# Turning attention weights by transposing transfers, with the pairs of heads spread over gates and u

## The chip, the cores and the metric

The kernel runs on one core of one Trainium2 chip. Its time is the device time of one execution in microseconds (us), the median of three runs. The engines are TensorE (PE, with its weight loads as PEld), VectorE (DVE), ScalarE (ACT), GpSimd (POOL) and SyncE (SP), which only issues DMAs here. DMAs that GpSimd issues stand in POOL's queue.

## The reference

Two layers, each of which is `x <- LN(alpha*x + 0.5*SwiGLU_1(x))`, `x <- LN(alpha*x + Mixer(x))`, `x <- LN(alpha*x + 0.5*SwiGLU_2(x))`, for 256 tokens of 1024 numbers, in float32. The change touches the mixer:

```python
z = x @ w_in
u, v, q, k, val, gates = jnp.split(z, SPLITS, axis=-1)
u, v = gelu(u), gelu(v)
# branch A: LN(v), then per group g of 8 a lower triangular 128x128 product over the positions of a chunk
s = jnp.einsum('gtr,bnrgc->bntgc', w, vb) + b_s.T[None, None, :, :, None]
h_a = u * s
# branch B: 8 heads, two softmaxes each; q and k of 64, val of 128 per head
q, k = rope(q), rope(k)
p = softmax(where(causal, q @ k.T * 64 ** -0.5, neg))
a = p[:, :, 0] - lam * p[:, :, 1]
o = a @ val
h_b = rmsnorm(o, diff_ln_g) * (1.0 - lam_init)
g = sigmoid(gates + gate_b)
m = g[:, :, 0] * (h_a @ w_branch[0]) + g[:, :, 1] * (h_b @ w_branch[1])
return m @ w_out
```

## The kernel before

**Precision.** Every large product runs in float32r with the weights cut into a high and a low part. `stream` (line 150) loads 1 MB of weights (128 x 2048) into one of four `raw` buffers; ACT writes the high part `whi` (line 169), DVE the low part `wlo` (line 171), in pieces of 1024 columns, of which eight buffers each exist. Activations stand as a high and a low half in one tile of 512.

**TensorE's order.** The order on TensorE is the order in which the program is written (`manual_schedule`); the other engines' orders are made by a scheduler from priorities, which grow with the order of the program, and from its own model of the times. `issue_after` (in `behind`) puts an instruction behind a named one on its engine: `emptied` is the last eviction of a bank on ACT, `added` the last addition of two halves on DVE, `turned_by` the last rope product on POOL, `loaded` the last load of weights on SP.

**Beats and side tasks.** Small work is written as generators beside the large products. `beat(w)` (line 123) advances a clock; a task whose due time has come runs up to its next `yield d`, and is due again d later, at the next beat that reaches it. `beside(task, delay)` enters a task. `gemm_a2` (line 234) takes one or two loads; for each of its loads it runs two pieces of eight 512-wide matmuls with the high part (line 244), with a beat of 0.65 after each piece, and then for each piece eight 256-wide matmuls with the low part (line 251) and a beat of 0.35. One load is thus two beats. `gemm_b` (line 273) advances the clock by 0.5 for every six matmuls (line 232).

**The mixer** (line 572) has these stages. `val` first; then four pairs of heads, each with a product for q and one for k and `rope` behind each; then eight products for the gates, one v (two halves), four u, then the products with the branch weights, `branch(1, hb)` and `branch(0, ha)`, of eight loads each, and `w_out`. Beside them:

- `attend(hp, qT, kT)` (line 607), one task per pair of heads, entered when its k is done with a delay of 4.5. `scores` uses four `side` banks, two for the second 128 tokens and two for the first. DVE and ACT make the two softmaxes, `less` (line 639) subtracts them on DVE. After 2.9 beats TensorE transposes the weights (lines 658 and 663), six blocks of 128 x 128 in two side banks, ACT evicts them to `aT`. After 1.9 more TensorE multiplies by the values (lines 671 and 673) into one side bank, ACT copies it to `on` (line 676) and squares the bank in place for the sums of the norm (line 681). POOL works out the reciprocal roots (`rsqrt4`, line 214), ACT scales `on` (line 690).
- `transposed` (line 175) turns `on`: POOL parts the two 16-bit halves of the numbers into two planes (line 186), SP issues one transposing DMA per plane (line 190), POOL joins the planes (line 194). ACT and DVE then write high and low part of `hb` (lines 700 and 702).
- `spatial(gp, uu)` (line 750), entered three beats after each u: four products per group pair into one side bank (line 756), then DVE adds the bias and multiplies by u (lines 761 and 763), ACT and DVE split the result into `ha` (lines 197 and 198).
- After v, DVE normalises `vg` (lines 735 and 737). POOL's queue loads `sgug` and `sgub` (line 407), `wsT` and `bsb` (lines 743 and 746), and POOL clears the upper triangle of `wsT` (line 744).

There are four `main` banks for the large products and four `side` banks. Tiles of 512 columns come from one pool, `act`, of 27 slots.

Of the kernel before, what the change touches and what calls it, by code (L numbers as in the profile page):

```python
# [20 lines left out]
P = 128  # L21
# [32 lines left out]
def trunk(ctx, tc, x, xT, w13a, w13b, w2, wb, wqk, wa, wbr, wo, gateb, sgug, sgub, sguwT, sgubias, lam, diffg,  # L54
# [41 lines left out]

    def t512(s, n=2):
        return tmp.tile([P, 512], F32, tag="main", name=name(s), bufs=n)
# [75 lines left out]

    def transposed(src, out, via, first, second):

        def planes(v):
            return v.bitcast(U16).rearrange("p (w c) -> p w c", w=2)  # L180

        def numbers(v):
            return v.bitcast(U16).rearrange("p (c w) -> p w c", w=2)

        for w in range(2):
            G.tensor_copy(out=planes(out)[:, w], in_=numbers(src)[:, w])  # L186
        yield first
        with behind(loaded[0]):
            for w in range(2):
                nc.sync.dma_start(planes(via)[:, w].rearrange("p (k t) -> p k t", k=4), planes(out)[:, w],  # L190
                                  transpose=True)
        yield second
        for w in range(2):
            G.tensor_copy(out=numbers(out)[:, w], in_=planes(via)[:, w])  # L194

# [321 lines left out]
    def ffn(l, f, i, norm, last=False):  # L517
# [18 lines left out]
        def turned(n, t, s, p, wait):  # L536
            yield from transposed(s, p[:, 0], p[:, 1], wait, 0.6)
# [34 lines left out]
    def mixer(l, i, norm):  # L572
# [13 lines left out]

        def rope(src, scale, last=False):

# [10 lines left out]
            def rest():  # L599
                with behind(None if last else added[0]):  # L600
                    V.tensor_tensor(out=r, in0=r, in1=sw, op=ALU.add)
                yield 0

            beside(rest(), 1.25 if last else 1.55)
            return r

        def attend(hp, qT, kT):
# [30 lines left out]

            def less(t, pp):

                nk = (t + 1) * P
                for j in range(2):
                    s = slice(j * nk, (j + 1) * nk)
                    V.scalar_tensor_tensor(out=pp[0][:, s], in0=pp[1][:, s], scalar=c4[:, t * 2 + j : t * 2 + j + 1],
                                            in1=pp[0][:, s], op0=ALU.mult, op1=ALU.add)
                return pp[0]

# [3 lines left out]
            V.scalar_tensor_tensor(out=c4, in0=rc, scalar=neg_lam[l], in1=sums[:, :4], op0=ALU.mult, op1=ALU.mult)  # L651
            second, first = less(1, second), less(0, first)
            yield 2.9
            b = side_bank()
            for j in range(2):
                for c in range(2):
                    o = (j * 2 + c) * P
                    PE.transpose(b[:, o : o + P], second[:, o : o + P], ident)  # L658
            aT1 = slots("aT", 2)[0]
            A.activation(aT1, b, AF.Copy)  # L660
            b = side_bank()
            for j in range(2):
                PE.transpose(b[:, j * P : (j + 1) * P], first[:, j * P : (j + 1) * P], ident)  # L663
            aT0 = slots("aT", 2)[0][:, :T]
            A.activation(aT0, b[:, :T], AF.Copy)
            yield 1.9
            b = side_bank()
# [11 lines left out]
            for q in range(4):  # L679
                s = slice(q * P, (q + 1) * P)  # L680
                A.activation(b[:, s], b[:, s], AF.Square, accum_out=ss[:, q : q + 1])
            yield 2
            with behind(turned_by[0]):
                G.tensor_tensor(out=ss, in0=s2, in1=ss, op=ALU.add)
            r = rsqrt4(ss, 1.0 / (2 * HD))
            yield 2
            for q in range(4):
                s = slice(q * P, (q + 1) * P)
                with behind(emptied[0]):
                    A.activation(on[:, s], on[:, s], AF.Copy, scale=r[:, q : q + 1])  # L690
            yield 1
            moved = slots("moved", 2)[0]
            yield from transposed(on, moved, on, 10, 0.3)
            yield 0.3
            dl = dgs[:, l : l + 1]
            for j in range(2):
                hi, lo = (hb[hp * 2 + j][:, o : o + T].rearrange("p (t c) -> p t c", t=NT) for o in (0, T))
                f = moved.rearrange("p (t j c) -> p j t c", t=NT, j=2)[:, j]
                with behind(emptied[0]):
# [5 lines left out]
        for hp in range(HEADS // 2):  # L705
            qT = rope(wqk[l, hp, 0], HD ** -0.5)
            kT = rope(wqk[l, hp, 1], 1.0, hp == HEADS // 2 - 1)
# [12 lines left out]

        vg = [act.tile([P, 2, 512], F32, tag="val", name=name("vg"), bufs=2) for _ in range(NT)]
        vst = [sm("vst", 12, bufs=2) for _ in range(NT)]
        for h in range(2):
# [3 lines left out]
            gemm_b(wb[l, V_, h], KT, xh, xl, got_v)  # L727
        g_bc, b_bc = bc_load(sgug[l], vst[0][:, :1]), bc_load(sgub[l], vst[0][:, :1])
        for t in range(NT):
            mv = sm("mv", 2)  # L730
            V.bn_aggr(out=mv, in_=vst[t])
            r = rsqrt(mv[:, 1:2], EPS)
            for h in range(2):
                s = slice(h * 512, h * 512 + 512)
                V.scalar_tensor_tensor(out=vg[t][:, h], in0=vg[t][:, h], scalar=mv[:, 0:1], in1=g_bc[:, s],
                                        op0=ALU.subtract, op1=ALU.mult)
                V.scalar_tensor_tensor(out=vg[t][:, h], in0=vg[t][:, h], scalar=r, in1=b_bc[:, s],
                                        op0=ALU.mult, op1=ALU.add)
        wsT, bsb = slots("wsT", 4), slots("bsb", 4)
# [9 lines left out]

        def spatial(gp, uu):  # L750
            b = side_bank()
# [11 lines left out]
            V.tensor_tensor(out=s1, in0=s1, in1=uu, op=ALU.mult)  # L763
# [122 lines left out]
```

## Time and profile before

| | |
|---|---|
| median of three runs | 1224.38 us (1224.3 to 1224.41) |
| time of the profiled execution | 1224.37 us |
| its span, from the first to the last instruction | 1222.4 us |
| granted clock of TensorE | 1.0 |
| busy PE, DVE, ACT, POOL | 99%, 72%, 58%, 22% of the span |

How to read it: L12 is line 12 of the kernel. A timeline row has start and length in us, the engine, the line, the operation, the names out<-in, the shape and the number of instructions merged; in brackets stands the idle time of the engine before it and what ended that. A group row ends in busy us, mean ns of one instruction, and the idle time before them. Matmuls overlap in the array and their ends are modelled, so two starts give a truer interval than a length. A row of DMAs ends in the median us from issue to landing. A window row has the length, then the busy us and number of instructions of PE, PEld, DVE, ACT and POOL, the granted clock, the share of the DMA engines' time and GB/s.

### The profile page before, as it was taken

The page shows a single profiled execution, that of the slowest core. Times are in us where ns is not written, and L with a number is a line of the kernel's source. Part 1 is how long each engine was busy: PE and PEld are TensorE (multiplying, and loading weights), DVE is VectorE, ACT ScalarE, POOL GpSimd, SP SyncE. Part 2 cuts the span into 40 slices and gives each one's busy share as a digit, 9 for nine tenths or more (in the row PEclk, how much of TensorE's full clock was granted, in tenths as well). Part 3 has the DMA queues.
Part 4 walks back from the last instruction along what each step waited for, and adds up shares of the span by engine and source line. Part 5 has one row for each costly group of instructions (what it writes and reads, how often), then busy time and mean ns, then how long its engine had stood idle before and what let it go on. Part 6 is the DMA issues. An engine that isn't in the chain of part 4 may idle for free.

```text
span 1222.4 us, 17217 instructions
## 1 busy us (share of the span) xinstructions
PE 1216.0 (99%) x6127; PEld 1030.1 (84%) x6127; DVE 884.9 (72%) x1500; ACT 710.8 (58%) x1356; POOL 271.8 (22%) x376
## 2 busy tenths in 40 slices
PE   9999999999999999999999999999999999999998
PEld 7888888888888888888888888888888888888887
DVE  7676767886787986766676766678867879676763
ACT  7475446678765555554455564466886655564740
POOL 1433000246400024230023320002462000323200
PEclk9999999999999999999999999999999999999999
DMA  9976645655853746867546757556568456577550
GB/s 345 307 217 231 245 174 185 229 176 169 283 198 138 249 155 215 245 203 258 195 159 205 258 181 258 207 185 204 170 191 277 146 179 235 173 235 238 183 187 35
DMA packets 92902, 254.43 MB, mean 208 GB/s; under 512 B 57568, under 2 KB 58640, under 8 KB 66704
## 3 DMA queue, kind: packets, MB, share of 16 engines
q1 hardware_dynamic: 88848, 240.68, 58.7%
q0 software_dynamic: 3536, 12.13, 3.0%
q8 instruction: 48, 0.79, 0.3%
q10 hardware_dynamic: 432, 0.52, 0.1%
q14 instruction: 38, 0.31, 0.1%
HBM read 235.47 MB, written 1.05 MB: 193 GB/s over the span
## 4 chain that ended last, share of the span: by engine, by line
PE 99%; DMA 0%; DVE 0%; ACT 0%; issue 0%; ACTq 0%
PE bank L232 64%; PE bank L244 19%; PE bank L251 10%; PE bank L347 2%; PE sbank L621 1%; PE sbank L498 1%; PE sbank L673 1%; PE sbank L756 1%; DMA xraw<-in_xT 0%; PE sbank L671 0%; PE sbank L658 0%; PE sbank L663 0%; PE sbank L470 0%; DVE xtok L478 0%; ACT whi L197 0%; DVE st L443 0%
## 5 line engine op out<-in xcount | busy, mean ns | idle before, releaser
L171 DVE TENSOR_TENSOR wlo<-raw,whi 128x512 fp32r<-128x512 f32 (+1 forms) x570 | 523.7, 954 | 137.9 <-ACT whi L169 80.9
L169 ACT ACTIVATE whi<-raw 128x512 fp32r<-128x512 f32 (+1 forms) x570 | 434.5, 800 | 252.5 <-PE bank L232 173.7
L232 PE MATMUL bank<-whi,x 128*128 128x512 f32 x1352 | 420.8, 390 | 0.0
L232 PEld LDWEIGHTS bank<-whi,x 128*128 128x128 f32 x1352 | 253.8, 188 | 52.5
L232 PE MATMUL bank<-wlo,x 128*128 128x512 f32 x676 | 263.1, 389 | 0.0
L244 PE MATMUL bank<-x,whi 128*128 128x512 f32 x768 | 184.6, 392 | 0.0
L244 PEld LDWEIGHTS bank<-x,whi 128*128 128x128 f32 x768 | 141.2, 188 | 28.5
L186 POOL COPY planes<-planes 128x512 uint16<-128x512 uint16 x80 | 85.6, 1096 | 309.0 <-DVE planes L530 309.0
L232 PEld LDWEIGHTS bank<-wlo,x 128*128 128x128 f32 x676 | 126.9, 188 | 26.1
L232 PE MATMUL bank<-whi,hhi 128*128 128x512 f32 (+1 forms) x374 | 141.2, 378 | 0.0
L232 PE MATMUL bank<-wlo,hhi 128*128 128x512 f32 (+1 forms) x374 | 141.0, 377 | 0.0
L232 PE MATMUL bank<-whi,hlo 128*128 128x512 f32 (+1 forms) x374 | 140.9, 377 | 0.0
L251 PE MATMUL bank<-x,wlo 128*128 128x256 f32 x768 | 103.1, 285 | 0.0
L251 PEld LDWEIGHTS bank<-x,wlo 128*128 128x128 f32 x768 | 98.5, 191 | 3.1
L194 POOL COPY planes<-planes 128x512 uint16<-128x512 uint16 x80 | 66.6, 878 | 106.8 <-DMA planes<-planes 106.3
L530 DVE TENSOR_TENSOR planes<-planes,bank 128x512 f32<-128x512 f32 x40 | 27.4, 684 | 87.0 <-issue 71.3
L529 ACT ACTIVATE planes<-bank 128x512 f32<-128x512 f32 x40 | 23.9, 598 | 103.7 <-PE bank L232 102.6
L232 PEld LDWEIGHTS bank<-whi,hhi 128*128 128x128 f32 x374 | 70.4, 188 | 12.9
L232 PEld LDWEIGHTS bank<-wlo,hhi 128*128 128x128 f32 x374 | 70.4, 188 | 12.8
L232 PEld LDWEIGHTS bank<-whi,hlo 128*128 128x128 f32 x374 | 70.4, 188 | 12.8
L597 POOL TENSOR_TENSOR swap<-swap,sin_t 128x512 f32<-128x512 f32 x16 | 27.1, 1692 | 239.8 <-DMA swap<-z 238.1
L252 ACT ACTIVATE r<-bank 128x256 f32<-128x256 f32 x128 | 47.5, 376 | 27.4 <-PE bank L251 27.2
(182 smaller groups left out, 1275.5 us busy)
## 6 DMA issues: line engine op xcount, KB each, us to landing
raw<-in_w13b SPq DMA_DIRECT2D x76, 1024.0 KB, 5.4
raw<-in_w SPq DMA_DIRECT2D x40, 1024.0 KB, 6.3
raw<-in_wa SPq DMA_DIRECT2D x24, 1024.0 KB, 5.6
raw<-in_wb SPq DMA_DIRECT2D x16, 1024.0 KB, 5.0
raw<-in_wqk SPq DMA_DIRECT2D x16, 1024.0 KB, 4.9
raw<-in_wbr SPq DMA_DIRECT2D x16, 1024.0 KB, 5.0
raw<-in_w13a SPq DMA_DIRECT2D x8, 1024.0 KB, 5.2
raw<-in_wo SPq DMA_DIRECT2D x8, 1024.0 KB, 5.0
```

The costliest lines, as they stand in the source:

```text
L169: A.activation(h, r, AF.Copy)
L171: V.tensor_tensor(out=w, in0=r, in1=h.bitcast(F32), op=ALU.subtract)
L186: G.tensor_copy(out=planes(out)[:, w], in_=numbers(src)[:, w])
L194: G.tensor_copy(out=numbers(out)[:, w], in_=planes(via)[:, w])
L232: PE.matmul(ps, xx, w, start=start and n == 0, stop=stop and n == 2)
L244: PE.matmul(b[-1], hi[:, k * P : (k + 1) * P], xc(k), start=k == 0, stop=False)
L251: PE.matmul(b[n][:, :T], lo[:, k * P : (k + 1) * P], xc(k)[:, :T], start=False, stop=k == KT - 1)
L252: emptied[0] = A.activation(r[:, s], b[n][:, T:], AF.Copy, scale=scale).ins
L347: PE.matmul(ps[t][m], x[:, j, o + t * P : o + (t + 1) * P], y, start=k0 + j == 0 and o == 0 and y is hi, stop=k0 + j == KT - 1 and y is lo)
L529: silu[0] = A.activation(s, ps[0], AF.Silu).ins
L530: added[0] = V.tensor_tensor(out=s, in0=s, in1=ps[1], op=ALU.mult).ins
L597: turned_by[0] = G.tensor_tensor(out=s3, in0=s3, in1=s, op=ALU.mult).ins
```

## The change

- The weights of attention are no longer transposed by TensorE. `less` writes into new tiles d1 (512 wide) and d0 (256), POOL parts them into planes (`parted`), SP issues two transposing DMAs for each (`moved`), and ACT joins the planes into `aT` (`joined`, written out with `A.activation`).
- The waits between the steps of `attend` are new, and the delay with which a pair's task is entered is 4.5 + 2.1 * hp, so that the pairs are spread over the stages of gates, u and v.
- The join of `on` goes from POOL to DVE; the feed-forward's joins stay on POOL.
- Two of the four u come before v and two behind it. The normalisation of v becomes a task in four steps (`settle`), the spatial products are entered at the end of v with delays from 7.4 to 10.7, and so stand in branch 1. The loads of `sgug` and `sgub` hang on a number of the first gate tile in place of one of v.
- The `act` pool has 26 slots for 27, the `main` temporaries three buffers for two. The last key's `rope` has the same delay as the others.

```diff
-    act = ctx.enter_context(tc.tile_pool(name="act", bufs=27))
+    act = ctx.enter_context(tc.tile_pool(name="act", bufs=26))
...
-    def t512(s, n=2):
+    def t512(s, n=3):
...
+    def parted(src, out):
         for w in range(2):
             G.tensor_copy(out=planes(out)[:, w], in_=numbers(src)[:, w])
+    def moved(src, out):
+        for w in range(2):
+            nc.sync.dma_start(planes(out)[:, w].rearrange("p (k t) -> p k t", t=P), planes(src)[:, w], transpose=True)
+    def joined(src, out, eng):
+        for w in range(2):
+            eng.tensor_copy(out=numbers(out)[:, w], in_=planes(src)[:, w])
...
-            beside(rest(), 1.25 if last else 1.55)
+            beside(rest(), 1.55)
...
-            second, first = less(1, second), less(0, first)
+            d1, d0, aT1 = (slots(n, 2)[0] for n in ("d", "d", "aT"))
+            d0, aT0 = d0[:, :T], d0[:, T:]
+            less(1, second, d1)
+            less(0, first, d0)
             yield 2.9
-            b = side_bank()
-            for j in range(2):
-                for c in range(2):
-                    o = (j * 2 + c) * P
-                    PE.transpose(b[:, o : o + P], second[:, o : o + P], ident)
-            aT1 = slots("aT", 2)[0]
-            A.activation(aT1, b, AF.Copy)
-            b = side_bank()
-            for j in range(2):
-                PE.transpose(b[:, j * P : (j + 1) * P], first[:, j * P : (j + 1) * P], ident)
-            aT0 = slots("aT", 2)[0][:, :T]
-            A.activation(aT0, b[:, :T], AF.Copy)
-            yield 1.9
+            with behind(turned_by[0]):
+                for d, a in ((d1, aT1), (d0, aT0)):
+                    parted(d, a)
+            yield 2
+            for d, a in ((d1, aT1), (d0, aT0)):
+                moved(a, d)
+            yield 3.6
+            with behind(emptied[0]):
+                for d, a in ((d1, aT1), (d0, aT0)):
+                    for w in range(2):
+                        A.activation(numbers(a)[:, w], planes(d)[:, w], AF.Copy)
+            yield 2
             b = side_bank()
...
-            yield 2
+            yield 0.8
             with behind(turned_by[0]):
                 G.tensor_tensor(out=ss, in0=s2, in1=ss, op=ALU.add)
             r = rsqrt4(ss, 1.0 / (2 * HD))
-            yield 2
+            yield 1.5
...
-            yield 1
-            moved = slots("moved", 2)[0]
-            yield from transposed(on, moved, on, 10, 0.3)
+            yield 0.4
+            onT = slots("onT", 2)[0]
+            parted(on, onT)
+            yield 1.6
+            moved(onT, on)
+            yield 2.2
+            with behind(added[0]):
+                joined(on, onT, V)
             yield 0.3
...
-            beside(attend(hp, qT, kT), 4.5)
+            beside(attend(hp, qT, kT), 4.5 + 2.1 * hp)
...
+        g_bc, b_bc = (bc_load(v[l], gates[0][0][:, :1]) for v in (sgug, sgub))
+        us = []
+        def u_part(gps):
+            for gp in gps:
+                uu = slots("u", 2)[0]
+                us.append(uu)
+                (_, uu), = gemm_a2([wa[l, U_, gp]], both, lambda m: uu)
+                A.activation(uu, uu, AF.Gelu)
+        u_part((0, 1))
...
-        g_bc, b_bc = bc_load(sgug[l], vst[0][:, :1]), bc_load(sgub[l], vst[0][:, :1])
+        def settle():
...
+                    yield 1
...
+        beside(settle(), 2.6)
         for gp in range(GROUPS // 2):
-            uu = slots("u", 2)[0]
-            (_, uu), = gemm_a2([wa[l, U_, gp]], both, lambda m: uu)
-            A.activation(uu, uu, AF.Gelu)
-            beside(spatial(gp, uu), 3)
+            beside(spatial(gp), 7.4 + 1.1 * gp)
+        u_part((2, 3))
```

More of the change, by code (lines that the diff above doesn't have):

```diff
@@ L173, in stream, with planes, numbers, transposed @@
         return out
[L175 to L183, printed above, removed]
+    def planes(v):
+        return v.bitcast(U16).rearrange("p (w c) -> p w c", w=2)
+    def numbers(v):
+        return v.bitcast(U16).rearrange("p (c w) -> p w c", w=2)
+    def parted(src, out):
         for w in range(2):
             G.tensor_copy(out=planes(out)[:, w], in_=numbers(src)[:, w])
+    def moved(src, out):
[4 more added lines that the diff above has]
+            eng.tensor_copy(out=numbers(out)[:, w], in_=planes(src)[:, w])
+    def transposed(src, out, via, first, second, eng):
+        parted(src, out)
         yield first
         with behind(loaded[0]):
-            for w in range(2):
-                nc.sync.dma_start(planes(via)[:, w].rearrange("p (k t) -> p k t", k=4), planes(out)[:, w],
-                                  transpose=True)
+            moved(out, via)
         yield second
-        for w in range(2):
-            G.tensor_copy(out=numbers(out)[:, w], in_=planes(via)[:, w])
+        joined(via, out, eng)
     def split(hi, lo, src):
@@ L536, in turned @@
         def turned(n, t, s, p, wait):
-            yield from transposed(s, p[:, 0], p[:, 1], wait, 0.6)
+            yield from transposed(s, p[:, 0], p[:, 1], wait, 0.6, G)
             x = p[:, 0].rearrange("p (k t) -> p k t", k=4)
@@ L585, in mixer, with rope @@
         hb = slots("hb", 2 * KT, F32R)
-        def rope(src, scale, last=False):
+        def rope(src, scale):
             (_, z), = gemm_a2([src], both, lambda m: slots("z", 2)[0], lambda: t512("r"), scale)
@@ L637, in exps, with less @@
                 return pp
-            def less(t, pp):
+            def less(t, pp, out):
                 nk = (t + 1) * P
@@ L690, in attend @@
                     A.activation(on[:, s], on[:, s], AF.Copy, scale=r[:, q : q + 1])
-            yield 1
-            moved = slots("moved", 2)[0]
-            yield from transposed(on, moved, on, 10, 0.3)
+            yield 0.4
[4 more added lines that the diff above has]
+            yield 2.2
+            with behind(added[0]):
+                joined(on, onT, V)
             yield 0.3
@@ L697, in attend @@
                 hi, lo = (hb[hp * 2 + j][:, o : o + T].rearrange("p (t c) -> p t c", t=NT) for o in (0, T))
[L698 removed]
+                f = onT.rearrange("p (t j c) -> p j t c", t=NT, j=2)[:, j]
                 with behind(emptied[0]):
@@ L748, in mixer, with spatial @@
         ha = slots("ha", 2 * KT, F32R)
-        def spatial(gp, uu):
+        def spatial(gp):
             b = side_bank()
@@ L762, in spatial @@
                                  in0=b.rearrange("p (j n t) -> p j n t", j=2, n=2)[:, :, t], in1=bias, op=ALU.add)
-            V.tensor_tensor(out=s1, in0=s1, in1=uu, op=ALU.mult)
+            V.tensor_tensor(out=s1, in0=s1, in1=us[gp], op=ALU.mult)
             for j in range(2):
```

27 lines of the change are left out of this document (13 added, 14 removed).

## The prediction

> **What bounds the kernel now.** The profile's page came first (span, busy shares, chain), then the chain of waits, the PE timeline of the mixer, the groups by shape, and last the ACT, DVE, POOL and SP timelines around each step that the change moves.
>
> ```profile
> span 1222.4 us, 17217 instructions
> PE 1216.0 (99%) x6127; PEld 1030.1 (84%) x6127; DVE 884.9 (72%) x1500; ACT 710.8 (58%) x1356; POOL 271.8 (22%) x376
> PE 99%; DMA 0%; DVE 0%; ACT 0%; issue 0%; ACTq 0%
> ```
>
> TensorE is busy for 99% of the span and the chain that ends last is TensorE for 99%. Its order is written out by hand, so a faster or slower step elsewhere changes the time only where TensorE comes to wait for it. The sum therefore has two kinds of terms: what leaves TensorE, and the new waits. The run with this profile took 1224.37 us, 1.97 us outside its span; the three runs have a median of 1224.38, so the two are one number. Under 0.2% (2.45 us) I call no change; that is about what a measurement of this kernel can tell.
>
> **What leaves TensorE.** Pair 0 of layer 0:
>
> ```profile
> 236.70 2.08 PE L251 MATMUL bank<-x,wlo 128*128 128x256 f32 x16
> 238.61 3.82 PE L244 MATMUL bank<-x,whi 128*128 128x512 f32 x16
> 242.27 1.12 PE L251 MATMUL bank<-x,wlo 128*128 128x256 f32 x8
> 243.22 0.60 PE L658 MATMUL sbank<-ident,pp 128*128 128x128 f32 x4
> 243.66 0.38 PE L663 MATMUL sbank<-ident,pp 128*128 128x128 f32 x2
> 243.79 1.20 PE L251 MATMUL bank<-x,wlo 128*128 128x256 f32 x8
> 244.83 2.00 PE L244 MATMUL bank<-x,whi 128*128 128x512 f32 x8
> ```
>
> Starts are the measure, since ends overlap. Sixteen lo matmuls without a break last 238.61 - 236.70 = 1.91 us; with the six transposes between them 244.83 - 242.27 = 2.56. A pair of heads thus pays 0.65 us, and four pairs in two layers 8 x 0.65 = 5.2 us. The other side products (scores, attention times values, spatial) keep their number and only change neighbours, which I cost at 0, within 0.3 either way.
>
> ```profile
> L658 PE MATMUL sbank<-ident,pp 128*128 128x128 f32 x32 | 4.8, 272 | 0.0
> L663 PE MATMUL sbank<-ident,pp 128*128 128x128 f32 x16 | 3.1, 272 | 0.0
> L660 ACT ACTIVATE aT<-sbank 128x512 f32<-128x512 f32 x8 | 4.8, 594 | 0.1
> L665 ACT ACTIVATE aT<-sbank 128x256 f32<-128x256 f32 x8 | 3.1, 385 | 0.0
> ```
>
> By mean durations the 48 transposes would be 48 x 0.272 = 13.1 us; they overlap in the array, so I take the starts. (The Trainium skill, TensorE: Matmul & The Clock Gate, Part 4: PE-mode transpose, has about 275 ns for one in a kernel's context. The duration agrees at 272; read as a cost it would give 13.2 us, where the starts show 5.2.)
>
> **What comes instead, off TensorE.** For each pair POOL parts d1 (two 128x512 copies) and d0 (two 128x256), SP issues four transposing transfers, ACT joins the halves with four copies; the join of `on` goes from POOL to DVE.
>
> ```profile
> L186 POOL COPY planes<-planes 128x512 uint16<-128x512 uint16 x80 | 85.6, 1096 | 309.0 <-DVE planes L530 309.0
> L186 POOL COPY moved<-on 128x512 uint16<-128x512 uint16 x16 | 12.1, 780 | 3.8 <-ACT on L690 3.8
> L194 POOL COPY moved<-on 128x512 uint16<-128x512 uint16 x16 | 15.1, 976 | 14.8 <-DMA on<-moved 14.8
> 278.93 2.53 SPq L190 DMA_TRANSPOSE on<-moved  x2
> planes<-planes SPq DMA_TRANSPOSE x80, 4.7
> on<-moved SPq DMA_TRANSPOSE x16, 2.3
> L454 DVE TENSOR_SCALAR xtok<-xtok,mv,nwy 128x512 f32<-128x512 f32 x20 | 10.0, 543 | 0.4
> ```
>
> POOL: 2 x 0.78 + 2 x about 0.4 (half as wide) = 2.4 us more, up to 3.3 at the 1.10 of the first row, and 2 x 0.98 = 2.0 less. SP: 2 x 1.27 + 2 x (0.6 to 1.27) = 3.8 to 5.1 us of issuing, then 2.3 to 4.7 to land. ACT: 2 x 0.59 + 2 x 0.385 = 2.0 in place of 0.98; no row shows ACT copying uint16, so I take the two evictions, the nearest by width. DVE: no row either; L454 with its 0.54 is the nearest (one wide input), so 1.1 more. In the new order a pair comes every 6 beats or so, some 17 us (a beat is worked out below), and none of this is a bound by itself.
>
> Three waits are new. SP's transfers wait for POOL's parting, with the weight loads behind them: at most 5.1 us of issuing and a copy's delay, while the four raw buffers hold four loads of 5.57 us of matmuls each, so 0. ACT's joins wait for the transfers, with conversions of weights and evictions of banks behind them; DVE's join likewise, with the low halves of the weights behind. Both are queued behind an eviction (`emptied`, `added`) that comes later than the transfer should land, so 0, and if a transfer is late, the converted weights (eight buffers of 1024, 22 us of matmuls) cover it.
>
> **Does TensorE wait for it?** Two products of a projection are 2 beats and 3.65 + 1.91 = 5.57 us, so a beat is 2.78 us; a step fires at the first beat past its due time. Counted from the mixer's first q, pair 0's k ends at 4, so its scores are due at 4 + 4.5 = 8.5 and fire at 8.65; 2.9 on, the parting fires at 11.65, 2 on the transfers at 13.65, 3.6 on the joins at 17.30, 2 on attention times values at 19.30. The old waits put transposes at 11.65 and the product at 13.65. All beats below are worked out so from the waits in the diff. `less` (L644) lies between:
>
> ```profile
> 246.77 1.58 PE L621 MATMUL sbank<-qk,qk 64*128 64x256 f32 x16
> 254.94 1.41 DVE L644 SCALAR_TENSOR_TENSOR pp<-pp,c,pp 128x256 f32<-128x256 f32 x4
> ```
>
> It ends 256.35 - 246.77 = 9.6 us after the scores start. From there the new path needs 3.3 (POOL) + 5.1 (SP) + 4.7 (landing) + 2.0 (ACT) = 15.1 us at the upper ends, 24.7 from the scores; the beats alone give 10.65 x 2.78 = 29.6, and other pairs' side products between only add to that. Cover: 4.9 us. Without it TensorE stands still for the difference, and behind it in its order stand the gates' matmuls. I take 0; the price past the cover is rival 4.
>
> The u stage is cut around v: the same loads on SP's queue in another order, the same eight products, so 0. Gelu's table comes at u in place of v:
>
> ```profile
> L725 ACT ACT_TABLE_LOAD x2 | 2.6, 1283 | 0.0
> ```
>
> Pair 3's exponentials follow scores at beat 27.30 and the first u ends at 34, so there is still one load a layer; a mix-up would cost ACT 2 x 1.3 us there, where it has time. The loads of `sgug`, `sgub`, `wsT` and `bsb` on POOL's queue now hang on the first gate tile, not on v, and can be drawn forward past the pairs' work; POOL then stands at L744 until its load lands:
>
> ```profile
> 334.18 0.95 POOL L744 TENSOR_SCALAR_AFFINE_SELECT wsT<-wsT 128x512 f32<-128x512 f32 x1 [7.55 <-DMA wsT<-in_sguwT]
> ```
>
> Before, nothing stood behind these 7.55 us. Now pair 1's parting may, and its product has the cover of 4.9 us at upper ends: bounds 0 and 2.7 us a layer. With the middle values (2.4 + 4.4 + 3.5 + 2.0) the cover is 7.7, so I take 0. Slots: at the first spatial product `hb` 8, gates 8, `wsT` and `bsb` 4, u 3 and `ha` 2 make 25 of the 26, so none waits: 0. The third main buffer and the last key's plain delay (1.55 for 1.25 beats, with its scores at 10.8) take nothing away: 0.
>
> **Side banks.** Scores take all four side banks, and a product's bank is freed by its last square on ACT:
>
> ```profile
> 252.43 1.20 PE L251 MATMUL bank<-x,wlo 128*128 128x256 f32 x8
> 257.40 0.19 ACT L681 ACTIVATION_READ_ACCUMULATOR sbank<-sbank 128x1 f32 x1
> 295.22 1.20 PE L251 MATMUL bank<-x,wlo 128*128 128x256 f32 x8
> 301.37 0.19 ACT L681 ACTIVATION_READ_ACCUMULATOR sbank<-sbank 128x1 f32 x1
> ```
>
> The products ended where these L251 begin, so a bank is held 5.2 us (pair 0) to 6.3 us (pair 3) longer. The new order puts scores of pair 2 at beat 21.30, two beats after pair 0's product starts, and scores of pair 3 at 27.30, two after pair 1's. That is 5.57 us after the product ends, and about 1 us more until the fourth bank is written (two thirds of the 1.58 of L621): 6.6 us. It holds by 0.3 to 1.4 us. I take 0; bounds 0 and 1 us at each of four places.
>
> **The end of the chain.** Pair 3's `hb` is split at beat 46.65, branch 1 starts at 48; its last weights are used 1.4 us into it. In between lie a POOL stretch and the scaling:
>
> ```profile
> 301.64 0.20 POOL L684 TENSOR_TENSOR ss<-s,ss 128x4 f32<-128x4 f32 x1 [1.36 <-ACT sbank L681]
> 308.84 0.29 POOL L225 TENSOR_TENSOR nwy<-nwa,nwy 128x4 f32<-128x4 f32 x1
> 309.17 1.28 ACT L690 ACTIVATE on<-on,nwy 128x128 f32<-128x128 f32 x4 [0.67 <-POOL nwy L225]
> ```
>
> POOL takes 7.5 us (301.64 to 309.13). From the end of pair 3's product: 6.3 (squares) + 7.5 + 1.3 (scale) + 2.0 (parting) + 2.5 + 2.3 (transfer) + 1.1 (DVE) + 1.5 (split, an estimate: two ACT and two DVE instructions of 256 columns, which overlap) = 24.5 us. The product comes at 38.50, so 9.5 beats of 2.75 us + 1.4 = 27.5 us are there. Cover 3.0 us, or 0.6 if the transfer takes 4.7 to land; bounds 0 and 1 us a layer, I take 0.
>
> **Spatial products.** They fire at beats 51.65, 52.65, 53.95 and 54.95, branch 0 starts at 56: 1.05 beats (2.9 us) after the last one, and its seventh matmul (1.4 us later) reads that `ha`. So 4.2 us are left after it ends. Before:
>
> ```profile
> 349.66 0.89 PE sbank L756 x8
> 354.93 0.78 DVE L198 TENSOR_TENSOR ha<-sgu,ha 128x256 fp32r<-128x256 f32 x2
> 369.03 0.89 PE sbank L756 x8
> 372.63 0.75 DVE L198 TENSOR_TENSOR ha<-sgu,ha 128x256 fp32r<-128x256 f32 x2
> ```
>
> From the product's end to `ha` 3.5 us (369.92 to 373.38) to 5.2 us (350.55 to 355.71). Bounds 0 to 1.0 us a layer; I take 0.3, nearer to the later one, which already stands in branch 1. Two layers: 0.6 us.
>
> **Sum.** 1224.4 - 5.2 + 0.6 = 1219.8 us.
>
> **The rivals.** (1) *Side banks run out.* For: the gates' stage is where ACT is fullest,
>
> ```profile
> 264.00:275.00 11.00, 11.00 (x75) 10.05 (x74) 9.07 (x29) 10.02 (x37) 6.69 (x17) 1.00 0.48 142
> ```
>
> (the fourth busy figure is ACT: 10.0 of 11 us), and it gains 1 us a pair there. Against: the exponentials, which crowd ACT in that window, are spread out. From a hold of 6.6 us every further us costs 4; it passes the bound to slower at (5.2 + 2.45) / 4 = 1.9 us, a hold of 8.5. At 9 us: 1219.8 + 4 x 2.4 = 1229.4. Chance of this side 0.15.
>
> (2) *Small waits eat the gain.* The upper bounds of bank, `hb`, `ha` and POOL's stand add to 4 x 1 + 2 x 1 + 2 x 1 + 2 x 2.7 = 13.4 us, which will not all come; a third is 4.5, less the 0.6 counted: 1223.7. For: each cover is thin. Against: each of them was taken at upper ends. Chance 0.15.
>
> (3) *DVE becomes the bound through POOL.* L171 doubles beside a POOL product:
>
> ```profile
> 219.48 1.23 DVE L171 TENSOR_TENSOR wlo<-raw,whi 128x1024 fp32r<-128x1024 f32 x1 [1.94 <-issue]
> 221.19 1.30 POOL L597 TENSOR_TENSOR swap<-swap,sin_t 128x512 f32<-128x512 f32 x1 [89.12 <-DMA swap<-z]
> 221.28 2.28 DVE L171 TENSOR_TENSOR wlo<-raw,whi 128x1024 fp32r<-128x1024 f32 x1
> ```
>
> POOL gains only 0.4 us a pair, so 8 x (0.4 + 1.1) = 12 us of DVE work, in stages where the window above leaves it 1.9 of 11 us. If a third of it came through: 1223.8. Chance 0.02.
>
> (4) *The transfers don't hide.* Past the cover of 4.9 us each us costs 8, one for each pair; at 1 us: 1227.8. For: a landing of 4.7 is a median, not the longest. Against: with a pair every 17 us no two pairs' transfers meet. Chance 0.03. (The Trainium skill, VectorE: DVE Perf Modes, Rules for kernel authors, would keep a 128x128 transpose on TensorE where PSUM will do. By that rule the change loses; it counts the transpose, not whose time is spare.)
>
> **Numbers.** Forecast 0.65, rivals 0.15, 0.15, 0.02, 0.03. Range: below, the full 5.2 and 0.3 of neighbours, 1218.9; above, rivals 2 and 3 held with some 0.8 beyond them, 1224.6, which leaves out rivals 1 and 4, 0.18. Faster: the forecast and 0.05 of rivals 2 and 3, 0.70. Within 0.2%: the rest of those two, 0.12. Slower: 0.18. The likeliest case by itself runs from 1218.9 to 1221.5.
>
> **What would show it.** Right: no L658 and L663 in the page, PE instructions down by 48, the sixteen L251 of a projection in 1.91 us with no break, TensorE's timeline closed around the scores of pairs 2 and 3. Wrong: idle time of PE released by the squares (rival 1), by `aT` (4), by `hb` or `ha` at the starts of the branches (2).

## Result and the profile after

| | before | after |
|---|---|---|
| median | 1224.34 us (1224.11 to 1224.41, 4 runs) | 1231.81 us (1229.22 to 1231.99, 4 runs) |
| ratio | | 1.0056, 95% interval 1.0039 to 1.0074 |
| profiled execution, span | 1224.37, 1222.4 us | 1231.76, 1230.1 us |

The change makes the kernel 0.56% slower. The forecast was 1219.8 us with a range up to 1224.6, so both the sign and the range were wrong.

In the changed kernel's line numbers, the matmuls of the projections are L254 (hi) and L261 (lo), the eviction and the additions behind them are L262 and L264/L266, the least values of the scores L643, their exponentials L645, `less` L654 with its factor `c` in L661, the joins of the weights on ACT L677, attention times values L683 and L685, the scaling of `on` L702, POOL's parting L184 and the transposing transfers L189.

The busy line of the changed kernel's page:

```profile
PE 1216.0 (99%) x6079; PEld 1027.7 (84%) x6079; DVE 891.5 (72%) x1516; ACT 718.2 (58%) x1372; POOL 271.6 (22%) x392
```

TensorE's waits in the changed kernel (us in total, times, the longest):

```profile
PE sbank L683 <- ACT d L677: 4.2, 2, 2.6
PE bank L254 <- DVE z L264: 4.2, 2, 2.1
```

The 48 transposes are gone (6127 to 6079 instructions), yet TensorE's busy time is what it was: 1216.0 us. And two kinds of wait stand there that the kernel before does not have, each once a layer. Start to start, less one matmul (0.23 us), the four stops are 2.1 and 2.2 us ahead of the second projection of the first gate column (call it stop A), 1.8 and 2.7 us ahead of pair 3's products with the values (stop B): 8.8 us.

**Stop A.** The changed kernel's timeline of TensorE around it in layer 0 (start, length, what; in brackets idle time and what ended it), pair 1's scores and the late matmul, and then VectorE's and GpSimd's:

```profile
251.43 1.58 PE L631 MATMUL sbank<-qk,qk 64*128 64x256 f32 x16
264.61 1.65 PE L254 MATMUL bank<-x,whi 128*128 128x512 f32 x3 [2.08 <-DVE z L264]
```

```profile
249.26 1.07 DVE L611 TENSOR_TENSOR qk<-qk,swap 128x512 f32<-128x512 f32 x1 [1.19 <-POOL swap L607]
250.25 1.63 DVE L171 TENSOR_TENSOR wlo<-raw,whi 128x1024 fp32r<-128x1024 f32 x1
252.46 2.33 DVE L171 TENSOR_TENSOR wlo<-raw,whi 128x1024 fp32r<-128x1024 f32 x1
261.52 1.25 DVE L661 SCALAR_TENSOR_TENSOR c<-rc,neg_lam,sums 128x4 f32<-128x4 f32 x1
262.81 1.41 DVE L654 SCALAR_TENSOR_TENSOR d<-pp,c,pp 128x256 f32<-128x256 f32 x4
264.13 0.42 DVE L264 TENSOR_TENSOR z<-bank,r 128x256 f32<-128x256 f32 x1
```

```profile
249.17 1.63 POOL L184 COPY aT<-d 128x512 uint16<-128x512 uint16 x2
250.74 1.73 POOL L184 COPY d<-d 128x256 uint16<-128x256 uint16 x2
252.44 1.27 POOL L607 TENSOR_TENSOR swap<-swap,sin_t 128x512 f32<-128x512 f32 x1
261.04 1.71 POOL L607 TENSOR_TENSOR swap<-swap,sin_t 128x512 f32<-128x512 f32 x1 [7.33 <-DMA swap<-z]
```

The addition at 264.13 empties a main bank of k3, for which TensorE's next matmul waits. It could have run some 2 us earlier (experiment 6 shows it at 261.76); it stands on VectorE behind pair 1's `less`, which now falls into k3 since pair 1 comes 2.1 beats later. Above it, L611 takes 1.07 us and a correction of weights 1.63, beside POOL's new parting of pair 0 (249.17 to 252.47, the first two GpSimd rows). A second correction takes 2.33 and the factor of four numbers 1.25, each beside a rope product on POOL (L607, the third and fourth row), which the kernel before has too.

**Stop B.** ScalarE's timeline in the same layer, then pair 3's last transposing transfers on SP's queue and the first and last instruction of GpSimd's root:

```profile
323.34 1.28 ACT L702 ACTIVATE on<-on,nwy 128x128 f32<-128x128 f32 x4 [4.54 <-POOL nwy L235]
325.43 1.28 ACT L746 ACT_TABLE_LOAD   x1
329.69 1.40 ACT L677 ACTIVATE aT<-d 128x512 uint16<-128x512 uint16 x2
331.45 0.81 ACT L677 ACTIVATE d<-d 128x256 uint16<-128x256 uint16 x2
```

```profile
312.45 2.50 SPq L189 DMA_TRANSPOSE d<-aT  x2
```

```profile
317.08 0.20 POOL L696 TENSOR_TENSOR ss<-s,ss 128x4 f32<-128x4 f32 x1 [6.83 <-ACT sbank L693]
323.10 0.20 POOL L235 TENSOR_TENSOR nwy<-nwa,nwy 128x4 f32<-128x4 f32 x1
```

Pair 3's last transposing transfers were issued by 314.95, and the longest landing of such a transfer (tile aT) is 6.8 us, so they had landed by 321.8. The joins end at 332.26 because ScalarE first stood 4.54 us at pair 2's scaling, for POOL's root of four numbers (317.08 to 323.3), and then worked off what had queued up behind it, the table load for u's Gelu (1.28) among it. In layer 1 the same wait is 5.3 us.

**The clock.** Two of the four stops are followed by a granted clock of one half. Busy time by stretches, with the clock in the third column from the end:

```profile
261.01:264.42 3.41, 1.51 (x13) 1.31 (x11) 3.38 (x7) 3.41 (x7) 1.71 (x1) 1.00 0.90 363
264.42:267.83 3.41, 3.22 (x8) 2.55 (x9) 3.38 (x7) 1.05 (x3) 0.00 (x0) 0.50 0.74 286
936.84:940.25 3.41, 1.02 (x5) 0.52 (x3) 2.58 (x4) 3.41 (x8) 0.00 (x0) 1.00 0.10 23
940.25:943.66 3.41, 3.23 (x14) 3.16 (x15) 2.44 (x4) 2.17 (x4) 0.00 (x0) 0.50 0.86 308
```

In 3.41 us at half clock TensorE starts 8 and 14 matmuls (x8, x14), and reads as busy throughout. The one run of the four whose clock was 1.000 took 1229.22 us, 2.6 less than the median, so a halved stretch is worth some 1.3 us, an estimate from this one run. Together: 8.8 (stops) + 2.6 (clock) - 4.65 (the transposes, measured below) = 6.8 us, of 7.5 between the medians; 0.7 us stays unplaced.

### The profile page after: what moved, and what is told of

It is laid out like the page before. It is cut to its first block, busy times and chain, and to the rows that moved or that the text cites. A ratio compares the mean times of both kernels' runs of the same rounds, so it can differ in the third digit from the quotient of the medians.

```text
span 1230.1 us, 17231 instructions
## 1 busy us (share of the span) xinstructions
PE 1216.0 (99%) x6079; PEld 1027.7 (84%) x6079; DVE 891.5 (72%) x1516; ACT 718.2 (58%) x1372; POOL 271.6 (22%) x392
## 4 chain that ended last, share of the span: by engine, by line
PE 90%; ACT 4%; DVE 2%; issue 1%; DMA 1%; POOL 1%; SPq 0%; DVEq 0%; ACTq 0%; POOLq 0%
PE bank L242 63%; PE bank L254 15%; PE bank L261 7%; PE bank L357 2%; ACT whi L169 1%; ACT pp L645 1%; DVE wlo L171 1%; PE sbank L508 1%; PE sbank L786 1%; PE sbank L685 1%; DMA swap<-z 1%; PE sbank L631 0%; DMA raw<-in_wb 0%; DVE d L654 0%; PE sbank L369 0%
## 5 line engine op out<-in xcount | busy, mean ns | idle before, releaser
L254 PE MATMUL bank<-x,whi 128*128 128x512 f32 x768 | 185.6, 394 | 4.2 <-DVE z L264 4.2
L254 PEld LDWEIGHTS bank<-x,whi 128*128 128x128 f32 x768 | 142.5, 190 | 33.2 <-DVE z L264 4.6
L184 POOL COPY planes<-planes 128x512 uint16<-128x512 uint16 x80 | 84.4, 1082 | 314.1 <-DVE planes L540 314.1
L261 PEld LDWEIGHTS bank<-x,wlo 128*128 128x128 f32 x768 | 97.4, 191 | 3.3
L261 PE MATMUL bank<-x,wlo 128*128 128x256 f32 x768 | 99.8, 284 | 0.0
L193 POOL COPY planes<-planes 128x512 uint16<-128x512 uint16 x80 | 67.9, 894 | 101.5 <-DMA planes<-planes 101.1
L242 PEld LDWEIGHTS bank<-wlo,hhi 128*128 128x128 f32 x374 | 70.4, 188 | 12.8
L242 PEld LDWEIGHTS bank<-whi,hhi 128*128 128x128 f32 x374 | 70.4, 188 | 12.7
L607 POOL TENSOR_TENSOR swap<-swap,sin_t 128x512 f32<-128x512 f32 x16 | 26.6, 1661 | 245.2 <-DMA swap<-z 240.5
L262 ACT ACTIVATE r<-bank 128x256 f32<-128x256 f32 x128 | 46.4, 374 | 26.7 <-PE bank L261 26.1
```

Of the source, the lines that this page charges most:

```text
L193: eng.tensor_copy(out=numbers(out)[:, w], in_=planes(src)[:, w])
L242: PE.matmul(ps, xx, w, start=start and n == 0, stop=stop and n == 2)
L254: PE.matmul(b[-1], hi[:, k * P : (k + 1) * P], xc(k), start=k == 0, stop=False)
L261: PE.matmul(b[n][:, :T], lo[:, k * P : (k + 1) * P], xc(k)[:, :T], start=False, stop=k == KT - 1)
L262: emptied[0] = A.activation(r[:, s], b[n][:, T:], AF.Copy, scale=scale).ins
L607: turned_by[0] = G.tensor_tensor(out=s3, in0=s3, in1=s, op=ALU.mult).ins
```

## Experiments

All edits are against the changed kernel except where said. My theory was that the static order makes the stops: A by VectorE's, B by ScalarE's. The main rivals were the transfers, GpSimd's copies beside VectorE, and the order of u and v.

**1. Pair 1 earlier**

```
-            beside(attend(hp, qT, kT), 4.5 + 2.1 * hp)
+            beside(attend(hp, qT, kT), (4.5, 4.5, 8.7, 10.8)[hp])
```

> The changed kernel with pair 1 entered at 4.5 beats instead of 6.6 (pairs at 4.5, 4.5, 8.7, 10.8), all else as it is. Theory, order on VectorE: pair 1's scores go back from projection k3 to the end of q3, its subtraction is done before the additions that empty k3's banks come up, and the two stops of about 2.1 and 2.2 us ahead of the first gate column go, with the halved clock that followed the first of them (about 1.3 us): 1231.8 - 4.3 - 1.3 = 1226.2 us. The stops in v (1.8 and 2.7 us) stay. Rival, port: GpSimd's parting copies slow VectorE whatever the place; the stops stay near 2 us and the time near 1231.8. Rival, the spreading is needed for the side banks: a stop in q3 or k3 takes their place, 1231 or more.

1238.29 us, ratio 1.0114 (1.0097 to 1.0131). Stop A went, and others came in the gate columns. Its TensorE waits on the gates, then ScalarE's and VectorE's timelines ahead of the stop that ends at 306.89:

```profile
PE bank L254 <- DVE gz L264: 10.2, 4, 4.0
```

```profile
298.63 0.70 ACT L702 ACTIVATE on<-on,nwy 128x128 f32<-128x128 f32 x2 [5.20 <-POOL nwy L235]
302.51 0.49 ACT L645 ACTIVATE pp<-pp,mx 128x256 f32<-128x256 f32 x1
```

```profile
306.41 0.42 DVE L264 TENSOR_TENSOR gz<-bank,r 128x256 f32<-128x256 f32 x1
```

ScalarE stood 5.2 us for POOL's root again, this time with a pair's eight exponentials and the evictions of a gate column behind it. So the gain was lost to the same kind of wait at other places. Of the third expectation only the time came (1231 or more): the stops are not in q3 or k3, and no side bank is waited for. The run says nothing clean about stop A, since the shift moved the scores as well as `less`.

**2. Scaling later**

```
-            yield 1.5
+            yield 2.7
             for q in range(4):
...
-            yield 1.6
+            yield 1
             moved(onT, on)
-            yield 2.2
+            yield 1.6
```

> The changed kernel with each pair's scaling placed 1.2 beats later (1.5 to 2.7), and the two waits behind it shortened by as much in all (1.6 to 1, 2.2 to 1.6). Theory, order on ScalarE: ScalarE does pair 1's planes, the table load, u's Gelu and evictions before it stands for GpSimd's root, so pair 3's joins are done before TensorE comes to them; the stops in v (1.8 and 2.7 us) go, with the halved clock behind the second (about 1.3 us): 1231.8 - 4.5 - 1.3 = 1226.0 us. Rival, late transfers: the joins wait for the transposing DMAs, not for their place; the stops stay, 1231.8. Rival, the root is late for hb: the branch on hb stops instead, by up to 1.2 beats (about 4 us a layer): 1231 or more.

1225.16 us (1222.92 to 1226.78), ratio 1.0003 (0.9994 to 1.0013). ScalarE now goes through `hb`, the table load and u's Gelu before the scaling, and only stop A is left in TensorE's waits. ScalarE's rows of this kernel, and TensorE's wait:

```profile
325.46 0.99 ACT L702 ACTIVATE on<-on,nwy 128x128 f32<-128x128 f32 x3
327.17 1.41 ACT L677 ACTIVATE aT<-d 128x512 uint16<-128x512 uint16 x2
```

```profile
PE bank L254 <- DVE z L264: 3.4, 2, 2.1
```

**3. Both of these**

> Both edits together. Theory: no stop is left, no halved clock, and the six transposes taken from TensorE are seen whole: 1224.4 - 5.2 = 1219.2 us (1219 to 1220.5). Rival, the two stops hang together (taking one away lets the other grow): 1223 to 1227. Rival, the spreading or the order of u and v costs by itself: the sum of the single gains is not reached, 1222 or more without a visible stop.

1234.27 us, ratio 1.0084 (1.0069 to 1.0099): the stops of experiment 1 in the gates (4.6 us in three waits) and stops at pair products (4.9 us in three). No better than the changed kernel.

**4. A shorter root on GpSimd**

```
-        for e in (-26 / 27, -8 / 9, -2 / 3):
+        for e in (-2 / 3,):
```

> The changed kernel with one Newton step in place of three in GpSimd's root of four values: two refinements of the normalisation's factor are left out, the order in the code is kept. GpSimd's 15 instructions in 6.2 us become about 7, some 3 us shorter. Theory, ScalarE stands for the root: the stop of 1.8 to 2.7 us ahead of pair 3's products goes or falls below 0.3 us, and the halved clock with it; the stops ahead of the gates stay: 1226 to 1227 us. Rival, transfers or the evictions themselves: the stops in v stay as they are, 1231.8.

1226.21 us (1223.70 to 1228.61), ratio 1.0015 (1.0006 to 1.0025). The order in the code is kept; only GpSimd's chain is shorter. ScalarE's wait and the first join in this kernel:

```profile
321.68 1.28 ACT L702 ACTIVATE on<-on,nwy 128x128 f32<-128x128 f32 x4 [2.50 <-POOL nwy L235]
328.04 1.41 ACT L677 ACTIVATE aT<-d 128x512 uint16<-128x512 uint16 x2
```

The wait falls from 4.54 to 2.50 us, and stop B is gone. With experiment 2 its cause is shown from both sides: moving the wait and shortening it both remove the stop, and the transfers are the same in all three kernels (pair 3's last ones are issued by 314.95 in the changed kernel, 315.87 in experiment 2, 315.34 here).

**5. Only `less` of pair 1 later**

```
             second, first = exps(1, banks[0]), exps(0, banks[1])
+            if hp == 1:
+                yield 1.4
             V.reciprocal(out=rc, in_=sums[:, 4:])
...
-            yield 2.9
+            yield 1.5 if hp == 1 else 2.9
```

> The changed kernel with pair 1's subtraction alone (reciprocal, factor and four subtractions) placed 1.4 beats later, and the wait behind it 1.4 beats shorter, so that everything else of the pair keeps its place; in VectorE's order it now comes behind the two additions that empty k3's banks. Theory, order on VectorE: the stops ahead of the first gate column (2.1 and 2.2 us, one of them followed by a halved clock of 1.3 us) go, the two in v stay: 1231.8 - 4.3 - 1.3 = 1226.2 us. Rival, GpSimd's copies slow VectorE there whatever the order: stops near 2 us, 1231.8. Rival, as after the earlier entry of pair 1: the stop goes to another column, 1230 or more.

1227.92 us (1227.18 to 1229.86), ratio 1.0032 (1.0019 to 1.0044). Stop A is gone in both layers; a new one appears in the middle of pair 3's scores, which wait for a side bank that the squares free: 1.0 us in layer 0, 0.3 in layer 1. It is the wait of the prediction's rival 1. 3.9 us gained, 5.6 expected. From TensorE's waits:

```profile
PE sbank L631 <- ACT sbank L695: 1.2, 2, 1.0
```

**6. Both of the edits 2 and 5**

> Pair 1's later subtraction and the later scaling together: no stop of over 0.5 us left between the layers' ends, TensorE's clock full throughout, and the time is that of the six transposes taken away: 1224.4 - 5.2 = 1219.2 us (1218.8 to 1220.5), under both kernels. Rival, the two interact as the earlier entry of pair 1 did: a new stop of 1 us or more and 1222 or more.

1220.68 us (1220.25 to 1221.16, 5 runs), ratio 0.9968 (0.9956 to 0.9981): under both kernels. The busy line of its page, then VectorE's timeline at the place of stop A:

```profile
PE 1212.7 (100%) x6079; PEld 1025.5 (84%) x6079; DVE 887.4 (73%) x1516; ACT 716.6 (59%) x1372; POOL 280.0 (23%) x392
```

```profile
252.69 2.33 DVE L171 TENSOR_TENSOR wlo<-raw,whi 128x1024 fp32r<-128x1024 f32 x1
261.76 0.42 DVE L264 TENSOR_TENSOR z<-bank,r 128x256 f32<-128x256 f32 x1
264.70 1.40 DVE L654 SCALAR_TENSOR_TENSOR d<-pp,c,pp 128x256 f32<-128x256 f32 x4
```

The correction beside GpSimd still takes 2.33 us, but the addition runs at 261.76 in place of 264.13. No stop of over 0.5 us is left but the two at the very start and end (1.1 and 0.7 us) that the kernel before has too, and the clock is whole up to 1216.89. The gain is 3.8 us of the 4.65 that experiment 9 measures; the time lies 0.2 us above what was expected, and the rest of 0.9 us is not placed.

**7. Weights turned on TensorE again, at the changed places**

```
-            yield 2.9
...
+            yield 8.5
+            for d, a, n in ((d1, aT1, 4), (d0, aT0, 2)):
+                b = side_bank()
+                for o in range(0, n * P, P):
+                    PE.transpose(b[:, o : o + P], d[:, o : o + P], ident)
+                with behind(emptied[0]):
+                    A.activation(a, b[:, : n * P], AF.Copy)
             yield 2
```

> The changed kernel with its places for pairs, u, v and spatial products, but the weights turned on TensorE again: six transposes and two evictions a pair at the place of the joins, no parting on GpSimd and no transposing DMA for them. Theory, the order costs: the transposes' 5.2 us come back and the stops stay, near 2 us ahead of the gates and 1 to 2.7 in v: 1231.8 + 5.2 = 1237 us (1234 to 1238). Rival, the transposing transfers and their copies make the stops: they go, and the time is that of the kernel before, 1224 to 1226.

1238.50 us, ratio 1.0117 (1.0102 to 1.0133). The time is near the theory's 1234 to 1238, but not by its reason: neither stop A nor B is there. VectorE's timeline at the place of A and ahead of the new stop, and TensorE's wait:

```profile
249.00 0.69 DVE L611 TENSOR_TENSOR qk<-qk,swap 128x512 f32<-128x512 f32 x1 [1.20 <-POOL swap L607]
249.60 1.22 DVE L171 TENSOR_TENSOR wlo<-raw,whi 128x1024 fp32r<-128x1024 f32 x1
251.41 1.21 DVE L171 TENSOR_TENSOR wlo<-raw,whi 128x1024 fp32r<-128x1024 f32 x1
260.43 0.21 DVE L661 SCALAR_TENSOR_TENSOR c<-rc,neg_lam,sums 128x4 f32<-128x4 f32 x1
262.00 0.42 DVE L264 TENSOR_TENSOR z<-bank,r 128x256 f32<-128x256 f32 x1
...
351.09 0.80 DVE L193 COPY onT<-on 128x512 uint16<-128x512 uint16 x2 [7.50 <-DMA on<-onT]
```

```profile
PE bank L254 <- DVE u L264: 7.8, 3, 4.0
```

VectorE has the same order here, `less` ahead of the addition. In layer 0 it takes 262.00 - 249.00 = 13.00 us from L611 to the addition, against 264.13 - 249.26 = 14.87 in the changed kernel. TensorE's own way to this place counts from pair 1's scores: from there the addition starts after 10.5 us for 12.7 in layer 0 (scores at 251.46) and after 11.3 for 12.7 in layer 1 (863.54 and 874.84, in the changed kernel 860.02 and 872.75). So 2.2 and 1.4 us of the stops come with the parting and its transfers. Pair 0's six transposes, which stand on TensorE just ahead of the place here, take another 0.6 (260.48 to 261.06); in layer 1 the stop would not be gone without them.

The transfers have a part in this besides GpSimd's copies. On SP's queue the loads of `swap` stand behind them, in the changed kernel (first row) later than here (second row):

```profile
257.04 2.43 SPq L603 DMA_DIRECT2D swap<-z  x4
246.09 7.87 SPq L603 DMA_DIRECT2D swap<-z  x8
```

So the rope product that waits for the last of them comes at 261.04 there, beside the factor, which takes 1.25 us, and at 256.69 here, where the factor takes 0.21. My theory held half: the order lets the delay through (5 and 6), the work that the change gives to GpSimd and to SP's queue makes it. The new stops are again a queue: VectorE's join of `on` (L193, `behind(added[0])`) stands 7.5 us for a transfer that lands late, and the additions of u behind it.

**8. Old order of u, v and the spatial products**

```
-        u_part((0, 1))
...
-        beside(settle(), 2.6)
+        for _ in settle():
+            pass
         for gp in range(GROUPS // 2):
-            beside(spatial(gp), 7.4 + 1.1 * gp)
-        u_part((2, 3))
+            u_part((gp,))
+            beside(spatial(gp), 3)
```

> The changed kernel with v again ahead of all of u, the normalisation of v right behind it and each spatial product three beats behind its column of u; turning by transfers and spreading of the pairs as changed. Theory: the stops ahead of the first gate column stay (2.1 and 2.2 us, some 1.3 of halved clock), since they lie ahead of u and v; pair 3's joins no longer have u's table load and Gelus ahead of them but still stand behind pair 2's scaling, so a stop of 0 to 2.7 us a layer stays at pair 3's products: 1226 to 1232 us. Rival, the order of u and v is what costs: 1219 to 1222. Rival, the new order is needed for the spatial products and hb: new stops there, 1232 or more.

1255.03 us, ratio 1.0252 (1.0238 to 1.0266): the third expectation, and more. TensorE's waits, and VectorE's join of `on`:

```profile
PE bank L254 <- DVE u L264: 9.9, 2, 5.6
PE bank L254 <- DVE hb L719: 8.0, 2, 4.2
PE bank L254 <- DVE z L264: 3.8, 2, 2.1
```

```profile
340.80 0.80 DVE L193 COPY onT<-on 128x512 uint16<-128x512 uint16 x2 [7.25 <-DMA on<-onT]
```

Stop A is unmoved (the z row), stop B gone, and u's additions and `hb` are late: VectorE stands 7.25 us for the transfer of `on`. In the new order none of these two waits exists, so the moved u does not cost here; without it the spread pairs cost 23 us more.

**9. The kernel before without its transposes**

```
             yield 2.9
-            b = side_bank()
...
+            aT1, aT0 = second, first
             yield 1.9
```

> The kernel before with the six transposes a pair and their two evictions left out: the weights go into the products unturned. This measures the term of the sum that the change was to take from TensorE, without any of its other parts. By the sum: 1224.4 - 5.2 = 1219.2 us (1218.5 to 1219.8). Rival, the transposes lay under other waits of TensorE: above 1221.

1219.88 us (1219.06 to 1219.98), beside 1224.53 of before: 4.65 us, ratio 0.9962 (0.9947 to 0.9977). The first term of the sum was right within 0.6 us.

**10. Parting of pair 0 later**

```
-            yield 2.9
+            yield 2.9 if hp else 4
             with behind(turned_by[0]):
                 for d, a in ((d1, aT1), (d0, aT0)):
                     parted(d, a)
-            yield 2
+            yield 2 if hp else 0.9
```

> The changed kernel with pair 0's parting on GpSimd 1.1 beats later (its transfers keep their place), so that VectorE's weight corrections ahead of pair 1's scores no longer run beside it; pair 1's subtraction still stands ahead of the additions that empty k3's banks. Theory, parting and its transfers lengthen the chain and the order passes it on: the corrections go back from 1.6 and 2.3 us to 1.2, and the stops ahead of the gates shrink by about 1 us or go, with the halved clock behind one of them: 1226 to 1230 us. Rival, order alone: stops of 2.1 and 2.2 us as before, 1231.8.

1227.90 us (1226.81 to 1229.50), ratio 1.0027 (1.0017 to 1.0038). VectorE's timeline, then GpSimd's parting, now beside the least values, then TensorE's waits in the mixer:

```profile
250.28 2.36 DVE L171 TENSOR_TENSOR wlo<-raw,whi 128x1024 fp32r<-128x1024 f32 x2
254.05 0.42 DVE L643 CUSTOM_DVE_ANT_0 pp<-sbank,mask 128x256 f32<-128x256 f32 x1
260.04 1.41 DVE L654 SCALAR_TENSOR_TENSOR d<-pp,c,pp 128x256 f32<-128x256 f32 x4
261.36 0.75 DVE L264 TENSOR_TENSOR z<-bank,r 128x256 f32<-128x256 f32 x2
```

```profile
253.89 1.17 POOL L184 COPY aT<-d 128x512 uint16<-128x512 uint16 x2
```

```profile
PE sbank L683 <- ACT d L677: 5.4, 3, 2.6
```

The corrections are back at 1.18 us each, the additions come at 261.36 although `less` is still ahead of them, and stop A is gone. In layer 1 it is gone too. A third wait for the joins has come (0.6 us in layer 1). Two of k's additions now lie between the least values, and the next rope product comes at 264.34, behind the addition, so this run alone would not settle it. With experiment 7, where other things differ, it does: stop A needs both, VectorE's order and the delay that the parting and its transfers bring. How much of the delay is the copies' and how much the later rope product's is not shown.

## Why the prediction was wrong, by its steps

- **What leaves TensorE (-5.2 us): right.** 48 instructions fewer, 4.65 us by experiment 9. A transpose's 272 ns was not its price. The Trainium skill's rule (VectorE: DVE Perf Modes, Rules for kernel authors) to keep such a transpose on TensorE had the sign of this kernel right, but not for good: experiment 6 turns by transfers and is faster.
- **Sizes off TensorE: right within some tenths.** ACT's joins were put at 2.0 us a pair and took 2.2 (1.40 + 0.81); DVE's two copies of `on` were put at 1.1 and took 0.80. Only the landing went past its upper end: put at 2.3 to 4.7, its median is 3.2 and its longest 6.8 (tile aT).
- **"Both are queued behind an eviction (`emptied`, `added`) that comes later than the transfer should land, so 0": the step that failed for stop B.** The transfers did land in time, as written. But a queued instruction waits for all that stands ahead of it, and ahead of the joins I counted only the eviction, not the scaling, which itself waits for GpSimd. The old kernel's 0.67 us at that scaling was shown and given no term; it is 4.54 here, with the pauses ahead of it cut (2 to 0.8 and 2 to 1.5 beats), and with the scaling placed later the stop is gone (experiment 2). Price: 4.5 us and a halved clock.
- **The cover of 4.9 us, which has `less` end 9.6 us after the scores start: the step that failed for stop A.** For pair 1 it is 264.22 - 251.43 = 12.8 us. Attention's own products were still in time for this pair. What I did not ask is what stands behind `less` on VectorE: two additions that free main banks.
- **Rival 3 (DVE through POOL) was weighed as a sum and given 0.02.** Its mechanism was right and its unit wrong: VectorE was no bound (72% busy), but a delay of 1.4 to 2.2 us at one place came straight through, once a layer.
- **The granted clock was not in the sum.** By the estimate above it costs 2.6 us behind two of the four stops.
- **The sign of being wrong "by `aT` (4)"** named the symptom of stop B, but as one of late transfers. The additions of z were not on the list.
- **Right:** side banks (no stop in the changed kernel, 1.0 us in experiment 5), spatial products, `hb` and slots cost nothing visible. The 0.6 us for `ha` did not show. There is still one table load a layer, but at stop B its 1.28 us stands between the scaling and the joins; no run takes it out of there.

## What to carry to other kernels

When a step is moved or slowed, ask of each engine what stands directly behind it in program order and which bank that frees; an average share of busy time does not answer this. An instruction that may wait for a slow engine should stand behind everything that is ready, not ahead of it: two such moves turned 0.56% slower into 0.32% faster. And price a stop of TensorE at more than its length where the granted clock can fall behind it.

## What was not expected of the hardware

**The halved clock follows a grid.** In every trace its starts lie whole multiples of 3.413 us apart (264.42 and 940.25 in the changed kernel: 198 of them; up to 289 in others). I cut the ten traces with the change or parts of it into these windows and added up TensorE's idle time of each, start to start as above: behind each of the 16 windows at full speed with 2.1 us or more the next one was halved, behind one with 1.76 us or less never, and between 1.80 and 1.95 us it went either way (in the changed kernel, 1.95 us from 261.01 halved the next, 1.80 us from 329.28 did not). So the same stop costs some 1.3 us more or nothing, by where it falls: the changed kernel's stop of 2.2 us at 873.22 was cut by a border into 0.9 and 1.2 us and left the clock whole. This may be part of why runs of one kernel spread where a stop is near the bound: in experiment 2 the two runs with a mean clock of 1.000 took 1222.92 and 1223.54 us, the others up to 1226.78. It is not all of it, since a run of experiment 4 at 1.000 took 1226.40. The Trainium skill, TensorE: Matmul & The Clock Gate, Part 1, tells of a free-running window of 4096 cycles, about 3.4 us, and the runs agree. Its section "Why this matters for your kernels" asks for no gaps over about 3 us; here 2.1 us in one window were enough, so the measurement decides.

**GpSimd's work slows VectorE by the kind of its operands.** A correction with two operands in SBUF took 1.63 us for 1.2 beside the parting's copies and 2.33 beside a rope product, while the least values, one of whose operands lies in a PSUM bank, kept 0.42 beside the copies (experiment 10, the row at 254.05). The Trainium skill, SBUF — State Buffer, section "SBUF: two separate sides", has the two engines share a pair of ports as an exclusive lock, for VectorE's operations with two SBUF inputs; this agrees. That the lock and nothing else makes the delay was argued here, not tried.
